# RMSNorm with swish: a ring of 100 rows instead of 96, with the last 28 rows loaded in other pieces and released by other stores

## The chip, the core and the metric

The kernel runs on one NeuronCore of one Trainium2 chip. Such a core has several engines with an instruction stream each: TensorE (not used here), VectorE (DVE in the profile), ScalarE (ACT), GpSimd (POOL) and SyncE (SP). SP does no arithmetic; here it issues the loads. ACT computes and also issues the stores. Every load and every store runs on the same 16 DMA engines, and each of the two issuing engines has a DMA queue of its own: q1 holds SP's loads, q10 holds ACT's stores. Engines wait for each other and for transfers on semaphores.

The metric is the device time in microseconds. It is given as a median over runs. A profile shows one execution.

## The reference

Each row of 512 numbers is divided by its root mean square, multiplied by `gamma`, and put through swish:

```python
batch, seq, dim = 16, 1024, 512            # x is float32
rms = np.sqrt(np.mean(x ** 2, axis=-1, keepdims=True) + eps)
x_norm = x / rms * gamma
return (x_norm * (1.0 / (1.0 + np.exp(-x_norm)))).astype(np.float32)
```

There are 16,384 rows of 2 KB. The core reads 33.56 MB and writes 33.56 MB.

## The kernel before

**Layout.** The 16,384 rows lie on 128 partitions, 128 rows to a partition. Below, "row 40" means the 41st row of every partition; one such row over all partitions is 256 KB, four of them are 1 MB, sixteen are 4 MB. The rows come in eight `groups` of 16. The buffer `xb` holds `ring` = 96 rows in each partition, that is six groups; groups 6 and 7 (rows 96 to 127) use the places of groups 0 and 1 again, which `slots` says. Everything is done in place: a row is loaded, squared, scaled, put through swish and stored from the same place.

**Loads** are twelve DMAs in SP's program order (line 119). A piece is written (group, first row in the group, number of rows). Pieces 0 to 8 fill the ring and wait for nothing: 4, 4, 8, 16, 16, 16, 16, 12 and 4 rows. The first two are issued ahead of the start barrier (`early`). Pieces 9, 10 and 11, of 16, 12 and 4 rows, go to places that were used before, so `load` makes SP wait (line 117) until the rows that stood there are stored: piece 9 waits for stores 0 and 1 (the second through `behind`), piece 10 for nothing further, piece 11 for store 2.

**Stores** are ten DMAs in ACT's program order (line 193): 16, 12, 4, then five of 16, then 8 and 8 rows. Each waits for the swish of its last rows. Two of them are also held back: `hold` makes ACT itself wait (line 191) for a landing. Store 0 stands at chunk 12 of ACT's loop and waits for load piece 7, rows 80 to 91. Store 3 stands at chunk 22 and waits for load piece 10, rows 112 to 123. Each time the four rows of one more load piece are still to come. Since the wait is an instruction of ACT's stream, everything behind it on ACT waits too.

**The computation** goes in K = 32 chunks of four rows (`cn`). For chunk k:

- ACT (`square`, lines 161 to 171) waits for the load piece that the chunk begins, squares two rows with a running sum (tile `junk`) and two rows into `sq`.
- DVE (`sums`, line 217) sums `sq`. POOL (lines 145 and 152) adds eps and takes the power of minus one half.
- DVE (`norm`, line 228) multiplies the four rows by it and by `gamma`, one row at a time.
- ACT (`swish`, line 183) applies swish to the four rows.

The order on ACT is written out by hand. In round k of its loop it issues `square(k)`, then every store that is due (two rounds after its last rows' chunk, and not before the round that `hold` names), then `swish(k - 2)`. ACT's instruction stream runs ahead of its arithmetic by a few instructions, so a store of round k can be issued while arithmetic of round k - 1 still runs.

At the end SP waits (line 250) for the stores that it has not waited for yet.

Of the kernel before, what the change touches and what calls it, by code (L numbers as in the profile page):

```python
# [9 lines left out]
def kernel(  # L10
# [8 lines left out]
    P = nc.NUM_PARTITIONS  # L19
# [6 lines left out]
    R, D = xf.shape  # L26

    groups = [16] * 8
    slots = [0, 16, 32, 48, 64, 80, 0, 16]
    loads = [(0, 0, 4), (0, 4, 4), (0, 8, 8)]  # L30
    loads += [(g, 0, 16) for g in range(1, 5)]
    loads += [(5, 0, 12), (5, 12, 4), (6, 0, 16), (7, 0, 12), (7, 12, 4)]
    stores = [(0, 0, 16), (1, 0, 12), (1, 12, 4)]
    stores += [(g, 0, 16) for g in range(2, 7)]
    stores += [(7, 0, 8), (7, 8, 8)]
    hold = {0: (loads.index((5, 0, 12)), 12), 3: (loads.index((7, 0, 12)), 22)}
    behind = {loads.index((6, 0, 16)): 1}
    ring = 96
    early = 2
    cn = 4  # L40
    n_sq = 2

    first = [sum(groups[:g]) for g in range(len(groups))]
    assert P * sum(groups) == R, R
    assert all(s + n <= ring for s, n in zip(slots, groups))

    chunks = []
    for i, (g, r, n) in enumerate(loads):
        for c in range(r, r + n, cn):
            chunks.append((slots[g] + c, i if c == r else None))  # L50
    K = len(chunks)
    assert K * cn * P == R

    ends = [-(-(first[g] + r + n) // cn) for g, r, n in stores]

    inv_d = 1.0 / float(D)
    eps_f = float(eps)
# [4 lines left out]
    def sbuf(name, shape, dt=fp32):  # L62
        return nc.alloc_sbuf_tensor(name, shape, dt).ap()

    xb = sbuf("xb", [P, ring, D])
    gamma4 = sbuf("gamma4", [P, D])
    gamma_sb = sbuf("gamma_sb", [P, D])
    neg_half = sbuf("neg_half", [P, cn])
    ms = sbuf("ms", [P, K, cn])
    aeps = sbuf("aeps", [P, K, cn])  # L70
    rstd = sbuf("rstd", [P, K, cn])
    sq = [nc.alloc_psum_tensor(f"sq{i}", [P, n_sq, D], fp32).ap() for i in range(2)]
# [20 lines left out]
    def need(ins, sem, value):  # L93
        return ins.wait_op(sem, value, "sem-ge")

    def dram(ap, piece):
        g, r, n = piece
        rows = ap[P * first[g] : P * (first[g] + groups[g])]
        return rows.rearrange("(p n) d -> p n d", n=groups[g])[:, r : r + n, :]

    def place(piece):
        g, r, n = piece
        return slots[g] + r, slots[g] + r + n

    def buf(piece):
        a, b = place(piece)
        return xb[:, a:b, :]

    stored_by_sync = set()

    def load(i):
        a, b = place(loads[i])
        for u, piece in enumerate(stores):
            c, d = place(piece)
            over = piece[0] < loads[i][0] and c < b and a < d
            if (over or behind.get(i) == u) and u not in stored_by_sync:
                nc.sync.wait_ge(st[u], 16)
                stored_by_sync.add(u)
        return nc.sync.dma_start(  # L119
            out=buf(loads[i]), in_=dram(xf, loads[i])  # L120
        ).then_inc(ld[i], 16)
# [3 lines left out]
    for t in range(early):  # L125
        ins = load(t).ins
        assert here[-1] is ins or here[-1].name == ins.name
        here.pop()
        at = next(
            i for i, other in enumerate(entry)  # L130
            if other.engine == mybir.EngineType.SP
            and isinstance(other, mybir.InstDrain)
        )
        entry.insert(at, ins)
    for t in range(early, len(loads)):
        load(t)
# [5 lines left out]
    nc.gpsimd.wait_ge(s_half, 1)  # L142
    for k in range(K):
        need(
# [11 lines left out]
        ).then_inc(s_rstd, 1)  # L156

    def square(k):
        at, landing = chunks[k]
        if landing is not None:  # L160
            nc.scalar.wait_ge(ld[landing], 16)  # L161
        for j in range(n_sq, cn):
            n = k * (cn - n_sq) + j - n_sq
            acc = nc.scalar.activation(  # L164
                out=junk[n % 2], in_=xb[:, at + j, :], func=AF.Square,
                scale=inv_d**0.5, accum_out=ms[:, k, j : j + 1],
            )
            if n >= 2:
                need(acc, s_acc, n - 1)
            acc.then_inc(s_acc, 1)  # L170
        square = nc.scalar.activation(  # L171
            out=sq[k % 2], in_=xb[:, at : at + n_sq, :],
            func=AF.Square, scale=inv_d**0.5,
        )
        if k >= 2:
            need(square, s_sum, k - 1)
        square.then_inc(s_sq, 1)

    def swish(k):
        at, _ = chunks[k]  # L180
        rows = xb[:, at : at + cn, :]
        need(
            nc.scalar.activation(out=rows, in_=rows, func=AF.Silu), s_norm, k + 1  # L183
        ).then_inc(s_swish, 1)
# [4 lines left out]
    def store(t):  # L189
        if t in hold:  # L190
            nc.scalar.wait_ge(ld[hold[t][0]], 16)  # L191
        need(
            nc.scalar.dma_start(out=dram(of, stores[t]), in_=buf(stores[t])),  # L193
            s_swish, ends[t],
        ).then_inc(st[t], 16)
# [9 lines left out]
    stored = 0  # L205
    for k in range(K + 3):
        if k < K:
            square(k)
        while stored < len(stores) and max(ends[stored] + 2, after(stored)) <= k:
            store(stored)  # L210
            stored += 1
        if 2 <= k < K + 2:
            swish(k - 2)
# [8 lines left out]
        ).then_inc(s_sum, 1)  # L222

    def norm(k):
        at, _ = chunks[k]
        for j in range(cn):
            row = xb[:, at + j, :]
            ins = nc.vector.scalar_tensor_tensor(  # L228
                out=row, in0=row, scalar=rstd[:, k, j : j + 1], in1=gamma_sb,
                op0=ALU.mult, op1=ALU.mult,  # L230
            )
            if j == 0:
                need(ins, s_rstd, k + 1)
        ins.then_inc(s_norm, 1)

    for k in range(K + 1):
        if k < K:
            sums(k)
        if k == 0:
            need(  # L240
                nc.vector.stream_shuffle(gamma_sb, gamma4, [0] * 32), s_gld, 16  # L241
            ).then_inc(s_gamma, 1)
        if k == 1:
            nc.vector.wait_ge(s_gamma, 1)
        if k >= 1:
            norm(k - 1)
# [39 lines left out]
```

## Time and profile before

| what | value |
|---|---|
| median of three runs | 160.73 us (160.39 to 161.25) |
| span of the profiled execution | 159.0 us |
| what lies around the span, median less span | 1.7 us |
| DVE busy | 124.4 us (78%) |
| ACT busy | 129.6 us (82%) |
| POOL busy | 65.4 us (41%) |
| loads, q1 | 33.56 MB, 49.8% of the 16 engines' span |
| stores, q10 | 33.57 MB, 49.2% |
| mean DMA rate over the span | 422 GB/s |

The page gives no time of the profiled execution other than its span, so the 1.7 us is the difference between the median and that span.

How to read it: a row of the page in tenths shows the busy share in 40 equal slices of 3.98 us. The chain of work is followed back from the last instruction, each step to what released it; in it, "issue" is time in which an engine waited for nothing that the profile shows, "another core or an unknown queue" is a wait whose releaser was not found, ACTq is ACT's instruction stream (here it issues DMAs), ACT its arithmetic. "DMA to landing" counts from the issue of a DMA to the moment when the last of its bytes is reported landed. In the answer on stretches of time, a DMA packet counts in the stretch in which it starts, so that short stretches can show a share over 1.

### The profile page before, as it was taken

The page shows a single profiled execution, that of the slowest core. Times are in us where ns is not written, and L with a number is a line of the kernel's source. Part 1 is how long each engine was busy: PE and PEld are TensorE (multiplying, and loading weights), DVE is VectorE, ACT ScalarE, POOL GpSimd, SP SyncE. Part 2 cuts the span into 40 slices and gives each one's busy share as a digit, 9 for nine tenths or more (in the row PEclk, how much of TensorE's full clock was granted, in tenths as well). Part 3 has the DMA queues.
Part 4 walks back from the last instruction along what each step waited for, and adds up shares of the span by engine and source line. Part 5 has one row for each costly group of instructions (what it writes and reads, how often), then busy time and mean ns, then how long its engine had stood idle before and what let it go on. Part 6 is the DMA issues. An engine that isn't in the chain of part 4 may idle for free.

```text
span 159.0 us, 507 instructions
## 1 busy us (share of the span) xinstructions
DVE 124.4 (78%) x162; ACT 129.6 (82%) x193; POOL 65.4 (41%) x71
## 2 busy tenths in 40 slices
DVE  0129999999999990299999999999999999994000
ACT  0946999999999913999999999999999999947000
POOL 2035555555555550055555555555555555550000
DMA  7999999999999999989899999999999999999997
GB/s 262 441 489 396 420 486 412 396 470 453 389 422 433 433 400 433 503 367 470 363 410 396 455 408 416 443 495 420 396 462 447 412 404 478 437 396 453 387 441 301
DMA packets 3324, 67.16 MB, mean 422 GB/s; under 512 B 500, under 2 KB 500, under 8 KB 504
## 3 DMA queue, kind: packets, MB, share of 16 engines
q1 hardware_dynamic: 1728, 33.56, 49.8%
q10 hardware_dynamic: 1592, 33.57, 49.2%
q14 instruction: 4, 0.03, 0.0%
HBM read 33.56 MB, written 33.56 MB: 422 GB/s over the span
## 4 chain that ended last, share of the span: by engine, by line
ACT 65%; DMA 12%; issue 5%; DVE 4%; ACTq 2%; another core or an unknown queue 2%; SPq 0%
ACT xb L183 27%; ACT junk L164 22%; ACT sq L171 16%; DMA xb<-in_x_dram 12%; DVE xb L228 3%; ACTq L193 2%; DVE ms L217 1%; SPq L119 0%; ACTq L191 0%; ACTq L161 0%
## 5 line engine op out<-in xcount | busy, mean ns | idle before, releaser
L228 DVE SCALAR_TENSOR_TENSOR xb<-xb,rstd,gamma_sb 128x512 f32<-128x512 f32 x128 | 87.2, 744 | 0.0
L183 ACT ACTIVATE xb<-xb 128x2048 f32<-128x2048 f32 x32 | 60.9, 1902 | 10.4 <-issue 6.3
L217 DVE TENSOR_REDUCE ms<-sq 128x2 f32<-128x1024 f32 x32 | 39.1, 1223 | 17.7 <-ACT sq L171 14.5
L145 POOL TENSOR_SCALAR aeps<-ms 128x4 f32<-128x4 f32 x32 | 20.6, 644 | 71.9 <-DVE ms L217 71.9
L152 POOL TENSOR_TENSOR rstd<-aeps,neg_half 128x4 f32<-128x4 f32 x32 | 44.0, 1376 | 2.7
L164 ACT ACTIVATE junk<-xb 128x512 f32<-128x512 f32 x64 | 37.2, 582 | 3.2 <-DMA xb<-in_x_dram 3.2
L171 ACT ACTIVATE sq<-xb 128x1024 f32<-128x1024 f32 x32 | 32.2, 1005 | 0.0
L164 ACT ACTIVATION_READ_ACCUMULATOR junk<-xb 128x1 f32 x64 | 11.9, 187 | 0.0
L204 ACT ACT_TABLE_LOAD x1 | 1.3, 1283 | 3.6 <-issue 3.6
L241 DVE LOAD_MASK_SELECT gamma_sb<-gamma x1 | 0.0, 14 | 2.8 <-DMA gamma<-in_gamma_dram 2.8
L139 POOL MEMSET blank<- 128x16 f32 x1 | 0.1, 112 | 1.5 <-POOLq L60 1.5
L241 DVE STREAM_SHUFFLE gamma_sb<-gamma 128x512 f32<-128x512 f32 x1 | 0.7, 717 | 0.0
L140 POOL MEMSET gamma<- 128x512 f32 x1 | 0.5, 524 | 0.0
L267 POOL MEMSET const-float32-0.0<- 128x1 f32 x1 | 0.1, 98 | 0.2 <-issue 0.2
L267 POOL MEMSET const-uint8-127<- 128x1 uint8 x1 | 0.1, 102 | 0.0
L267 POOL MEMSET const-bfloat16-1.0<- 128x1 bf16 x1 | 0.1, 101 | 0.0
L141 POOL MEMSET neg_half<- 128x4 f32 x1 | 0.1, 101 | 0.0
L267 POOL MEMSET const-float32-1.0<- 128x1 f32 x1 | 0.1, 98 | 0.0
## 6 DMA issues: line engine op xcount, KB each, us to landing
out_dram<-xb ACTq DMA_DIRECT2D x6, 4096.0 KB, 19.2
xb<-in_x_dram SPq DMA_DIRECT2D x5, 4096.0 KB, 28.8
xb<-in_x_dram SPq DMA_DIRECT2D x2, 3072.0 KB, 37.0
xb<-in_x_dram SPq DMA_DIRECT2D x4, 1024.0 KB, 13.3
out_dram<-xb ACTq DMA_DIRECT2D x2, 2048.0 KB, 13.0
out_dram<-xb ACTq DMA_DIRECT2D x1, 3072.0 KB, 19.0
xb<-in_x_dram SPq DMA_DIRECT2D x1, 2048.0 KB, 10.3
out_dram<-xb ACTq DMA_DIRECT2D x1, 1024.0 KB, 19.8
```

Of the source, the lines that this page charges most:

```text
L140: nc.gpsimd.memset(gamma4, 0.0).then_inc(s_zero, 1)
L145: nc.gpsimd.tensor_scalar(out=aeps[:, k, :], in0=ms[:, k, :], scalar1=eps_f, scalar2=None, op0=ALU.add,),
L152: nc.gpsimd.tensor_tensor(out=rstd[:, k, :], in0=aeps[:, k, :], in1=neg_half, op=ALU.pow),
L164: acc = nc.scalar.activation(out=junk[n % 2], in_=xb[:, at + j, :], func=AF.Square, scale=inv_d**0.5, accum_out=ms[:, k, j : j + 1],)
L171: square = nc.scalar.activation(out=sq[k % 2], in_=xb[:, at : at + n_sq, :], func=AF.Square, scale=inv_d**0.5,)
L183: nc.scalar.activation(out=rows, in_=rows, func=AF.Silu), s_norm, k + 1
L193: nc.scalar.dma_start(out=dram(of, stores[t]), in_=buf(stores[t])),
L204: nc.scalar.preload_act_table_set("silu_and_others")
L217: nc.vector.tensor_reduce(out=ms[:, k, 0:n_sq], in_=sq[k % 2], op=ALU.add, axis=mybir.AxisListType.X,),
L228: ins = nc.vector.scalar_tensor_tensor(out=row, in0=row, scalar=rstd[:, k, j : j + 1], in1=gamma_sb, op0=ALU.mult, op1=ALU.mult,)
L241: nc.vector.stream_shuffle(gamma_sb, gamma4, [0] * 32), s_gld, 16
L267: nc = _bacc.Bacc("TRN2", target_bir_lowering=False, num_devices=1)
```

## The change

The ring has 100 rows, and a row's place is its number modulo 100. Pieces of loads and stores are now written (first row, number of rows), and the code that turns a piece into places changes with that; `slots` and `chunks` are gone. What the program issues differs in this:

- Load pieces 0 to 6 are as before. Piece 7 is rows 80 to 95 (16 rows, before 12). Piece 8 is rows 96 to 99 (before 92 to 95). Both still wait for nothing. The rest is 28 rows (before 32): pieces of 12, 12 and 4 rows at 100, 112 and 124.
- Stores 0, 1 and 2 are 16, 8 and 8 rows (before 16, 12 and 4). Then come three of 16 rows as before, 16 rows (80 to 95), 4 rows (96 to 99), 12 rows (100 to 111), 8 and 8: eleven stores instead of ten.
- Load piece 9 still waits for stores 0 and 1, which are now 24 rows instead of 28; piece 11 still waits for store 2.
- Store 0 still stands at chunk 12 of ACT and waits for load piece 7, which now ends with row 95 instead of 91. Store 3 still stands at chunk 22 and waits for load piece 10, which ends with row 123 as before.

Instructions of DVE and POOL are the same. On ACT one store is added; the order of everything else stays.

```diff
-    slots = [0, 16, 32, 48, 64, 80, 0, 16]
-    loads = [(0, 0, 4), (0, 4, 4), (0, 8, 8)]
-    loads += [(g, 0, 16) for g in range(1, 5)]
-    loads += [(5, 0, 12), (5, 12, 4), (6, 0, 16), (7, 0, 12), (7, 12, 4)]
-    stores = [(0, 0, 16), (1, 0, 12), (1, 12, 4)]
-    stores += [(g, 0, 16) for g in range(2, 7)]
-    stores += [(7, 0, 8), (7, 8, 8)]
-    hold = {0: (loads.index((5, 0, 12)), 12), 3: (loads.index((7, 0, 12)), 22)}
-    behind = {loads.index((6, 0, 16)): 1}
-    ring = 96
+    ring = 100
+    loads = [(0, 4), (4, 4), (8, 8), (16, 16), (32, 16), (48, 16), (64, 16), (80, 16)]
+    loads += [(96, 4), (100, 12), (112, 12), (124, 4)]
+    stores = [(0, 16), (16, 8), (24, 8), (32, 16), (48, 16), (64, 16), (80, 16)]
+    stores += [(96, 4), (100, 12), (112, 8), (120, 8)]
+    hold = {0: ((80, 16), 12), 3: ((112, 12), 22)}
+    behind = {(100, 12): (16, 8)}
...
     def buf(piece):
-        a, b = place(piece)
-        return xb[:, a:b, :]
+        a, n = piece
+        at = a % ring
+        assert at + n <= ring, piece
+        return xb[:, at : at + n, :]
...
     def load(i):
-        a, b = place(loads[i])
-        for u, piece in enumerate(stores):
-            c, d = place(piece)
-            over = piece[0] < loads[i][0] and c < b and a < d
+        a, n = loads[i]
+        for u, (c, m) in enumerate(stores):
+            over = c + ring < a + n and a < c + m + ring
             if (over or behind.get(i) == u) and u not in stored_by_sync:
                 nc.sync.wait_ge(st[u], 16)
                 stored_by_sync.add(u)
...
     def square(k):
-        at, landing = chunks[k]
-        if landing is not None:
+        at = k * cn % ring
+        for landing in landings[k]:
             nc.scalar.wait_ge(ld[landing], 16)
```

More of the change, by code (lines that the diff above doesn't have):

```diff
@@ L43 @@
     first = [sum(groups[:g]) for g in range(len(groups))]
[L44 to L54, printed above, removed]
+    rows_each = sum(groups)
+    assert P * rows_each == R, R
+    assert ring % cn == 0
+    for pieces in (loads, stores):
+        assert [a for a, _ in pieces] == [
+            sum(n for _, n in pieces[:i]) for i in range(len(pieces))
+        ]
+        assert sum(n for _, n in pieces) == rows_each
+    K = rows_each // cn
+    hold = {t: (loads.index(piece), k) for t, (piece, k) in hold.items()}
+    behind = {loads.index(a): stores.index(b) for a, b in behind.items()}
+    landings, seen = [], 0
+    for k in range(K):
+        landings.append([])
+        while seen < len(loads) and loads[seen][0] < (k + 1) * cn:
+            landings[k].append(seen)
+            seen += 1
+    ends = [-(-(a + n) // cn) for a, n in stores]
     inv_d = 1.0 / float(D)
@@ L96, in dram @@
     def dram(ap, piece):
-        g, r, n = piece
+        a, n = piece
+        g = max(g for g in range(len(groups)) if first[g] <= a)
+        r = a - first[g]
+        assert r + n <= groups[g], piece
         rows = ap[P * first[g] : P * (first[g] + groups[g])]
         return rows.rearrange("(p n) d -> p n d", n=groups[g])[:, r : r + n, :]
-    def place(piece):
-        g, r, n = piece
-        return slots[g] + r, slots[g] + r + n
     def buf(piece):
-        a, b = place(piece)
-        return xb[:, a:b, :]
+        a, n = piece
+        at = a % ring
+        assert at + n <= ring, piece
+        return xb[:, at : at + n, :]
     stored_by_sync = set()
     def load(i):
-        a, b = place(loads[i])
-        for u, piece in enumerate(stores):
-            c, d = place(piece)
-            over = piece[0] < loads[i][0] and c < b and a < d
+        a, n = loads[i]
+        for u, (c, m) in enumerate(stores):
+            over = c + ring < a + n and a < c + m + ring
             if (over or behind.get(i) == u) and u not in stored_by_sync:
@@ L179, in swish @@
     def swish(k):
-        at, _ = chunks[k]
+        at = k * cn % ring
         rows = xb[:, at : at + cn, :]
@@ L224, in norm @@
     def norm(k):
-        at, _ = chunks[k]
+        at = k * cn % ring
         for j in range(cn):
```

## The prediction

> **What bounds the kernel now.** I read the page's slices first: which resource is busy all the time?
>
> ```profile
> span 159.0 us, 507 instructions
> DVE  0129999999999990299999999999999999994000
> ACT  0946999999999913999999999999999999947000
> DMA  7999999999999999989899999999999999999997
> ```
>
> The 16 DMA engines are busy in every slice; DVE and ACT pause near 57 to 62 us and stop near 147. So bytes set the time, as long as each next transfer is in a queue before the last one ends. The rate of a pure store stretch, from the answer on stretches (the last two numbers are DMA share and GB/s):
>
> ```profile
> 101.00:157.00 56.00, 42.63 (x56) 42.95 (x60) 21.29 (x21) 1.00 1.00 433
> 62.40:98.30 35.90, 30.96 (x40) 35.90 (x54) 16.36 (x16) 1.00 0.99 419
> ```
>
> At 433 GB/s one MB (1.049e6 bytes) takes 2.42 us and 4 MB take 9.69. The second line tells the other half: from 62.4 to 98.3 ACT is busy 35.90 of 35.90 us. In that stretch ACT has no idle time at all, so what delays its start delays its end.
>
> Next, where ACT and DMA meet. Line 191 is ACT's wait for a landing; it ended twice, at 59.0 and at 98.3. The chain of waits around both:
>
> ```profile
> L191 ACTq EVENT_SEMAPHORE  x2: 17/17/17, 59.0 to 98.3; - x2
> ...
> 55.21 0.91 ACT sq L171
> 56.12 2.88 another core or an unknown queue
> ...
> 59.08 0.34 ACTq L193
> ...
> 59.45 1.57 ACTq L193
> ...
> 61.07 1.28 ACTq L193
> ...
> 62.40 1.91 ACT xb L183
> ...
> 98.33 0.38 ACT xb L183
> ```
>
> ACT runs dry at 56.12 and waits until 59.00. That end is load 7's landing: it was issued at 4.42, and its DMA to landing is 54.6, so 59.0. Then ACT issues three stores (0.34, 1.57, 1.28 us) and computes again at 62.40. The second end of line 191, at 98.3, was not set by the DMA. The loads released near 78.5 are these two:
>
> ```profile
> L119 SPq DMA_DIRECT2D xb<-in_x_dram x2: 328/658/987, 78.5 to 78.9; - x2
> DMA to landing us min/median/max: 12.4/15.9/19.3
> ```
>
> The second, load 10, landed at 78.86 + 19.3 = 98.2. The first end shows a wait for landing ending 0.02 us after it; here it ends over 0.1 us after, together with the start of an ACT arithmetic instruction at 98.3. So ACT reached the second wait just after the landing, with nothing to spare, and store 3 went out at 98.37. Load 11 (1 MB, 2.42 us) was left in the queue; it landed at 80.90 + 19.8 = 100.7, which covered store 3's start.
>
> **The change part by part.**
>
> *ACT's first hold.* Load 7 now ends with row 95, 1 MB more ahead of the landing. Loads run at the same rate there (load 6, issued at 3.88 with 47.8 to landing, landed at 51.7 and load 7 at 59.0: 7.3 us for 3 MB), so it lands at 59.0 + 2.4 = 61.4. ACT still reaches the wait at 56.12, since everything ahead is unchanged. All of ACT behind it, and DVE and POOL which feed from ACT's squares, shift by 2.42 us: swish(10) starts at 64.8 instead of 62.40, if the three issues again take 59.08 to 62.40 = 3.3 us. Their sizes change from 12 and 4 rows to 8 and 8. The trace has no such pair there; the bounds are three quick issues (0.34 and 0.44 us as those at 98.37 and 98.75, in all about 1.2, ACT then late by only 2.42 − 2.1 = 0.3) and two at 1.57 (late by 2.7). I take 3.3 unchanged, because those are three issues in the same place in the same state of the queues.
>
> *DMA in that time.* Store 0 goes out at 61.5, with load 8 (1 MB) still in the queue as before; the DMA stays busy, cost nothing. If that cover were gone, it would cost about a start, 1 to 2 us.
>
> *Release of loads 9 to 11.* Stores 0 and 1 are 6 MB instead of 7, and start one MB later: 2.42 − 2.42 = 0, so SP is again released at about 78.4 (before, 78.49 was the first issue). But behind store 1 there is now store 2 with 2 MB (4.85 us) instead of 1 MB (2.42). Before, the stores ran out as the new loads began: store 2 landed at 61.07 + 19.8 = 80.9, and load 10, 7 MB later, at 98.2, where 7 × 2.42 = 16.96 would give 97.8. So 0.3 us or more was lost there, and I estimate at most 0.8 (the page's slices from 75.5 to 83.5 moved 363 and 410 GB/s: 93/433 × 3.98 = 0.85). The longer cover can win back between 0 and 0.8 us; I take 0.4 for load 10's landing: 97.8. SP's other waits lose nothing: load 11 needs store 2, landed near 83, while loads 9 and 10 (6 MB, 14.5 us) keep the queue full.
>
> *The second hold.* ACT's work from 62.4 to 98.3 has no idle time, and its instructions between are the same. So it comes to the wait for load 10 at 98.3 + 2.4 = 100.7; load 10 has long landed. Store 3 is issued at 98.37 + 2.42 = 100.8. Behind load 10 the DMA engines have only load 11, whose last bytes move at about 100.2 − 0.4 = 99.8 (the landing of 100.7 less about half a us for the report and the slower engines). Then the queues are empty until store 3's first bytes. This is the new stall.
>
> How long is it? The row for a DMA on idle engines is the kernel's first load, issued at 0.00:
>
> ```profile
> 0.50:1.00 0.50, 0.00 (x0) 0.00 (x0) 0.00 (x0) 1.00 0.00 0
> 1.00:1.50 0.50, 0.00 (x0) 0.00 (x0) 0.00 (x0) 1.00 1.45 246
> ```
>
> Nothing starts before 1.0 us. The load has 1 MB (2.42) and landed after 4.7 us, so 2.3 us of it are start, ramp and report. The ramp is the stretch from 1.0 to 2.0 at 246 and 197 GB/s, which loses 1 − 222/433 = 0.49 us; without it, 1.8 us.
>
> From store 3 on, 96 rows (24 MB, 58.1 us) remain to be stored in one queue. So the last landing comes at 100.8 + 1.8 + 58.1 = 160.7 without a ramp, at 161.2 with one, against 159.0: +1.7 or +2.2. The low end: if a store's start costs only its issue, 0.34 us instead of 1.0, it is +1.0. I take +1.9, between the first two, for the first load is the only row of a DMA on idle engines, but a ramp need not be the same for a store.
>
> The Trainium skill, page "DMA: Bandwidth & Descriptors", section "Specifications", puts first-byte latency on the sync and scalar path at about 0.6 us. The row above shows 1.0, and the row decides; by the page's figure the sum would be 0.4 us smaller.
>
> *After it.* No later store comes too late: the last one is issued at 146.8 + 2.4 = 149.2 and needs 2 × 2.42 + 2.3 = 7.1 us to land, 156.4, well before the end of the queue near 161; before, it took 12.2 us to land, 5 us of which were waiting. Store 6 is issued near 118.6, when the 12 MB of stores 3 to 5 last until 131. The eleventh store costs one issue of 0.34 us on ACT beside 5 us of slack: nothing. DVE and POOL ends are hidden the same way.
>
> *Sum.* +1.9 us, with nothing to add for the 0.4 us gained earlier, since store 3 waits for ACT and not for the loads. The span 159.0 becomes 160.9; with the 1.7 us around it, 162.6, or the median plus 1.9.
>
> **The rivals.**
>
> 1. *ACT is not late (not slower).* If the three issues behind the first hold are quick, 1.2 us in all instead of 3.3, ACT reaches the second wait at 98.6 and store 3 goes out at 98.7, with bytes from 99.7, when load 11 ends anyway. Then the time is 160.73 − 0.2 = 160.5, to 160.8. For it: 0.34 and 0.44 at 98.4. Against: 1.57 and 1.28 in the very place, and 0.99 for SP's second load at 78.86. It decides once the issues save over 1.5 us. Half of that saving gives 161.6.
> 2. *The mixed stretch is slow.* Store 2's 2 MB and loads 9 and 10 now run side by side for some us; the trace of before has hardly any such stretch. If load 10 landed later than 100.7, each us more would add one: at 102, 163.9. Against: it needs 3 us lost in about 10, and around 60 us, where load 8 and store 0 met, the three slices from 55.7 to 67.6 moved 400, 433 and 503 GB/s, no less than 433 in the mean. The skill's same page, section "Queues, rings and completion order", says that each DMA engine switches between queues packet by packet; that would cost order, not bytes, and no row here shows it.
> 3. *The new ring only moves bytes.* The DMA is always full and the lost 0.4 to 0.8 us comes back: 160.1. It needs ACT early as in 1, plus another us that the trace does not offer.
>
> **How the numbers follow.** About 0.5% (0.8 us) can be told from no change here. ACT late, with a hole: 80%, 161.8 to 163.2 (+1.0, and +2.2 with issues 0.3 longer), likeliest 162.6. Issues half as quick: 7%, near 161.6, on the border. Rival 1: 6%, 160.5 to 160.8. Rival 3: 3%, 160.1. Rival 2: 4%, 163.9. Slower by over 0.5% (above 161.5): 80 + 4 + half of 7, some 87; I give 0.85, since the base of 160.39 to 161.25 itself wanders. Same 0.10, faster 0.05. The range of 8 in 10 takes the ends of the unknown start and a little of the half-quick case: 161.6 to 163.4.
>
> **What would show it.** Line 191's first wait ends at 61.4, swish(10) starts near 64.8, line 191's second wait ends near 100.7, the rate falls to near zero in about 100 to 101.8, and it stays at 433 to the end. SP's first wait still ends near 78.4 and the dip at 80 is smaller. The prediction is wrong if the second hold ends near 98, or if the DMA shows no hole there.

## The result and the profile after

The changed kernel takes 162.24 us (162.15 to 162.32), the kernel before 160.56 us in the same comparison (160.18 to 161.25). The ratio is 1.0113, with a 95% interval of 1.0095 to 1.0132: slower by 1.7 us. The prediction was 162.6, range 161.6 to 163.4. The profiled execution itself took 162.3 us, with a span of 161.0.

The page of the changed kernel, its span and its slices (40 slices of 4.02 us; lines moved down by six, so line 191 is now 197, 193 is 199, 183 is 189, 119 is 125):

```profile
span 161.0 us, 509 instructions
DVE  0149979999999990099999999999999999995000
ACT  1947979999999900999999999999999999948000
DMA  7999999999999989999999997999999999999997
```

In the 15th and 16th slices (56.4 to 64.4 us) ACT has 0 and 0, where it had 1 and 3: its pause has grown. And the DMA row has a 7 in the 25th slice (96.6 to 100.6 us), where it had a 9. The account below rests on these two places. The waits at line 197 and the chain of waits around the first of them:

```profile
L197 ACTq EVENT_SEMAPHORE  x2: 17/17/17, 61.5 to 100.6; - x2
...
56.31 5.12 another core or an unknown queue
...
61.51 0.34 ACTq L199
...
61.89 1.49 ACTq L199
...
63.42 1.26 ACTq L199
...
64.72 1.91 ACT xb L189
```

The first wait ends at 61.5 instead of 59.0, since one more MB has to land; ACT's arithmetic starts again at 64.72 instead of 62.40. From there it has no gap:

```profile
64.70:100.60 35.90, 30.97 (x40) 35.88 (x54) 16.35 (x16) 1.00 0.98 409
```

It is busy for 35.88 of 35.90 us and comes to the second wait at 100.6 instead of 98.3. By then load 10 has been in place for 2 us. The same answer on stretches of 1 us shows what the DMA does meanwhile (last two numbers: DMA share and GB/s; a packet counts in the stretch in which it starts). First the kernel before, then the changed one:

```profile
98.00:99.00 1.00, 0.86 (x2) 1.00 (x2) 0.00 (x0) 1.00 1.02 434
99.00:100.00 1.00, 1.00 (x2) 1.00 (x1) 0.28 (x1) 1.00 1.69 721
100.00:101.00 1.00, 1.00 (x3) 1.00 (x4) 0.92 (x2) 1.00 0.46 197
```

```profile
99.00:100.00 1.00, 1.00 (x3) 1.00 (x5) 1.00 (x1) 1.00 0.78 328
100.00:101.00 1.00, 0.86 (x2) 1.00 (x2) 0.16 (x1) 1.00 0.06 25
101.00:102.00 1.00, 1.00 (x2) 1.00 (x1) 0.00 (x0) 1.00 1.23 524
```

Before, the big packets of the stores start from 99.6 on, on the heels of the last loads. After, the loads run out near 100, only 0.06 us of DMA work starts between 100 and 101, and the stores begin after 101. When each packet of the trace is spread evenly over its own duration, the bytes moved between 99 and 102 us are short of 433 GB/s by 1.62 us in the changed kernel and by 0.01 in the kernel before. So of the 2.0 us between the two spans this hole holds 1.6; another 0.3 is lost between 104 and 150.

### The profile page after: what moved, and what is told of

It reads as the page before. It is cut to its first block, busy times and chain, and to the rows that moved or that the text cites. A ratio compares the mean times of both kernels' runs of the same rounds, so it can differ in the third digit from the quotient of the medians.

```text
span 161.0 us, 509 instructions
## 1 busy us (share of the span) xinstructions
DVE 124.4 (77%) x162; ACT 129.6 (81%) x193; POOL 65.4 (41%) x71
## 4 chain that ended last, share of the span: by engine, by line
ACT 64%; DMA 12%; issue 5%; DVE 4%; another core or an unknown queue 3%; ACTq 2%; SPq 0%
ACT xb L189 27%; ACT junk L170 22%; ACT sq L177 16%; DMA xb<-in_x_dram 12%; DVE xb L234 3%; ACTq L199 2%; DVE ms L223 1%; SPq L125 0%; ACTq L197 0%; ACTq L167 0%
## 6 DMA issues: line engine op xcount, KB each, us to landing
xb<-in_x_dram SPq DMA_DIRECT2D x1, 2048.0 KB, 10.4
```

## The experiments

Theory A: ACT comes late to the second hold because the first hold ends 2.4 us later, and the DMA stands empty for that. Rival B: what costs the time lies in the new pieces, in the stretch where store 2 meets the loads, or in the ring.

**The first hold put back.** Ring, stores and releases stay as changed; load piece (80, 16) is cut so that the first hold can end with row 91 again.

```diff
-    loads = [..., (64, 16), (80, 16)]
-    loads += [(96, 4), (100, 12), (112, 12), (124, 4)]
+    loads = [..., (64, 16), (80, 12)]
+    loads += [(92, 4), (96, 4), (100, 12), (112, 12), (124, 4)]
-    hold = {0: ((80, 16), 12), 3: ((112, 12), 22)}
+    hold = {0: ((80, 12), 12), 3: ((112, 12), 22)}
```

> The changed kernel, with the load piece of rows 80 to 95 cut in two (80 to 91, 92 to 95) and the first hold put back on row 91; ring, stores and release of loads stay as changed. Theory A (ACT comes late to the second hold because the first hold ends 2.4 us later): the first hold ends near 59.0, the second near 98.6 on the landing of load (112, 12), no hole in the DMA, 160.4 to 160.9. Rival B (the new pieces and the stretch in which store 2 meets the loads cost the time): nothing comes back, 162.0 to 162.4.

Measured: 160.74 us against 160.46 for the kernel before in the same comparison, ratio 1.0022 (1.0008 to 1.0035). The holds end at 59.1 and 98.8. So 1.4 of the 1.7 us come back with the new ring, the new stores and the new releases all in place, and B falls, but for the remaining 0.3. The chain of waits of this run holds something that was not expected:

```profile
59.12 0.34 ACTq L199
59.50 0.44 ACTq L199
59.99 0.51 ACTq L199
60.54 1.91 ACT xb L189
```

The three issues take 1.4 us here instead of 3.2, so ACT starts again at 60.54, 1.9 us earlier than even in the kernel before. Its instruction stream then waits for load 10 at the second hold (98.7, hold over at 98.8). The run thus undoes more of ACT's lateness than the hold alone.

**The second hold one round earlier.** The first hold stays at row 95; ACT is as late as in the changed kernel, but its program comes to the second hold one chunk sooner.

```diff
-    hold = {0: ((80, 16), 12), 3: ((112, 12), 22)}
+    hold = {0: ((80, 16), 12), 3: ((112, 12), 21)}
```

> The changed kernel, with the second hold one round earlier in ACT's program (21 instead of 22); the first hold stays at row 95. Theory A: ACT's instruction stream reaches the second hold near 96.7, waits there for the landing near 98.6 while its arithmetic has work until 100.6, store 3 is issued near 98.7, the loads end near 100 and the stores follow without a hole: 160.4 to 160.9. Rival B: 162.0 to 162.4.

Measured: 160.66 against 160.46, ratio 1.0015 (1.0000 to 1.0029). The first hold ends at 61.5, ACT starts at 64.82, and the second hold ends at 98.7, with the landing. The stretches show the stores following the loads (to be read against the changed kernel's above):

```profile
99.00:100.00 1.00, 1.00 (x3) 1.00 (x5) 1.00 (x1) 1.00 0.93 393
100.00:101.00 1.00, 0.85 (x3) 1.00 (x2) 0.26 (x1) 1.00 1.29 549
```

One number in the program gives back 1.5 us. This separates the two halves of theory A: an ACT that is 2.4 us late costs no more by itself than the remaining 0.2 us (0 to 0.5 by the interval); the late store 3 costs the rest. Where the 0.2 comes from was not tested.

**A late store 3 in the kernel before.** Nothing new but the round of its second hold.

```diff
-    hold = {0: (loads.index((5, 0, 12)), 12), 3: (loads.index((7, 0, 12)), 22)}
+    hold = {0: (loads.index((5, 0, 12)), 12), 3: (loads.index((7, 0, 12)), 23)}
```

> The kernel before, with the second hold one round later (23 instead of 22), nothing else: the cost of a late store 3 by itself. Theory A: the hold ends near 102.3, the loads have ended near 100, store 3 is issued at 102.4 and the span is 102.4 + 60.24 (the distance from store 3's issue to the end in the changed kernel) = 162.6, that is 164.2 as a time. Rival B has no new pieces here: 160.6.

Measured: 164.12 (163.93 to 164.17) against 160.46, ratio 1.0229 (1.0212 to 1.0246). The old ring and the old pieces lose 3.7 us when store 3 alone is late. Its DMA stands still for the two whole microseconds after the loads:

```profile
100.00:101.00 1.00, 1.00 (x3) 1.00 (x4) 0.92 (x2) 1.00 0.06 25
101.00:102.00 1.00, 1.00 (x2) 1.00 (x3) 0.88 (x1) 1.00 0.00 0
102.00:103.00 1.00, 0.89 (x2) 1.00 (x2) 0.00 (x0) 1.00 0.00 0
```

**One issue less behind the first hold.** Store 2 goes out one round later, so that only two issues stand between the first hold and ACT's arithmetic.

```diff
-        while stored < len(stores) and max(ends[stored] + 2, after(stored)) <= k:
+        while stored < len(stores) and max(ends[stored] + 2, after(stored), {2: 13}.get(stored, 0)) <= k:
```

> The changed kernel, with store 2 issued one round later on ACT (13 instead of 12); both holds stay. Theory A: two issues instead of three stand behind the first hold, so ACT starts again near 63.4 instead of 64.7 and comes to the second hold near 99.4 instead of 100.6; the hole in the DMA shrinks from 1.7 to about 0.4 us: 160.8 to 161.2. If the lateness of ACT is not what is paid (rival B): 162.0 to 162.4. If the third issue costs ACT as much one round later: 162.0 to 162.4 too, with the second hold still at 100.6.

Measured: 161.06 against 160.30, ratio 1.0046 (1.0030 to 1.0062). ACT starts again at 63.37 and reaches the second hold at 99.3. So the time that ACT spends on issuing stores counts in the lateness like the wait itself.

Together the runs give the price of a late store 3. The first column is the end of the second hold, the last the difference of the medians of that comparison:

```
kernel                        second hold ends   against the kernel before
second hold at round 21             98.7            +0.2 us
first hold put back                 98.8            +0.3 us
store 2 one round later             99.3            +0.8 us
changed kernel                     100.6            +1.7 us
before, second hold at 23          102.6            +3.7 us
```

From 100.6 to 102.6 it is 2.0 us for 2.0 us. Between 98.8 and 100.6 it is lower (1.4 us for 1.8); that the last of the loads still covers part there is likely, but not shown. The ends of the holds come from one profiled execution each, which in the run with the first hold put back took 161.27 us against its median of 160.74. So differences of a few tenths between the upper rows mean little.

**How much store cover helps the turn to loads.** The prediction had hoped for 0.4 us from 2 MB of stores, instead of 1 MB, still queued when the loads are released (the cover, below). With the second hold at round 21 the DMA is the bound again, and a change there can show. Here load (100, 12) is released by store 0, so that 4 MB of stores are still queued; load (112, 12) is released by store 1.

```diff
-    hold = {0: ((80, 16), 12), 3: ((112, 12), 22)}
-    behind = {(100, 12): (16, 8)}
+    hold = {0: ((80, 16), 12), 3: ((112, 12), 21)}
+    behind = {}
```

> As the run with the second hold at round 21, and load (100, 12) released by store 0 alone (4 MB of stores still queued then), load (112, 12) by store 1. If the dip at the turn from stores to loads is a fixed price: as that run, 160.4 to 160.9. If it is the size of the store cover that decides it: 0.8 us less, 159.6 to 160.0. If a longer mixed stretch is slow: 161 or more.

Measured: 160.92 against 160.46, ratio 1.0033 (1.0019 to 1.0046). No gain: it is 0.3 us more than with the second hold at round 21 alone, and lies between what was expected of a fixed price and of a slow mixed stretch. The other direction, no cover at all, in the kernel before:

```diff
-    behind = {loads.index((6, 0, 16)): 1}
+    behind = {loads.index((6, 0, 16)): 2}
```

> The kernel before, with load piece 9 released by store 2 instead of store 1: no store is left in the queue when the loads are issued. Of the dip at the turn from stores to loads two readings are left. If the dip (0.9 us in the kernel before, with 1 MB of stores as a cover, and 0.9 us in the changed kernel, with 2 MB) is a price of the turn itself, it adds to the uncovered start of the loads (about 1 us from issue to first bytes, and about 0.7 for the report of store 2): 161.8 to 162.4. If the dip is only the part of the start that the cover does not hide, the whole start stands in its place, 1.7 instead of 0.9: 161.0 to 161.4.

Measured: 162.60 (162.55 to 162.72) against 160.20, ratio 1.0148 (1.0131 to 1.0165). That is 2.4 us, nearer to the additive reading and above its range. The stretch from 76 to 96 us in five kernels, in the order before (1 MB of cover), changed (2 MB), load released by store 0 (4 MB), no cover, and the first hold put back (2 MB again):

```profile
76.00:96.00 20.00, 19.41 (x26) 20.00 (x31) 10.29 (x11) 1.00 1.01 421
```

```profile
76.00:96.00 20.00, 19.38 (x26) 20.00 (x31) 10.25 (x11) 1.00 1.01 416
```

```profile
76.00:96.00 20.00, 19.38 (x26) 20.00 (x32) 10.24 (x11) 1.00 1.00 401
```

```profile
76.00:96.00 20.00, 19.42 (x26) 20.00 (x32) 10.28 (x11) 1.00 0.89 369
```

```profile
76.00:96.00 20.00, 19.42 (x26) 20.00 (x31) 10.26 (x11) 1.00 1.00 427
```

These rates have an error at their borders, since a packet counts where it starts. With each packet spread evenly over its own duration, the bytes moved between 76 and 96 us fall short of 433 GB/s by 0.87, 0.90, 1.41, 3.18 and 0.20 us. So 1 MB of cover hides most of the start of the loads, and in the changed kernel 2 MB hide no more: about 0.9 us stays. In the uncovered run the DMA stands nearly still for about 2 us, and then the loads still take some 2 us to come up to the full rate.

The last of the five does not fit a fixed price. It has the cover of the changed kernel and loses only 0.20 us here. But it loses 0.60 between 60 and 64 us, at the turn from loads to stores behind the first hold, where the kernel before loses 0.04 and the changed one 0.10. So neither turn has a price of its own in these runs, and what sets the two they do not settle.

**A more patient kernel before.** If ACT reaches the second hold with nothing to spare, the earlier round might help there too.

```diff
-    hold = {0: (loads.index((5, 0, 12)), 12), 3: (loads.index((7, 0, 12)), 22)}
+    hold = {0: (loads.index((5, 0, 12)), 12), 3: (loads.index((7, 0, 12)), 21)}
```

> The kernel before, with the second hold one round earlier (21 instead of 22). ACT was on time already, so theory A expects no change, 160.3 to 160.7; if some executions of the kernel before owe part of their time to an ACT that comes a little late, up to 0.3 us less.

Measured: 160.24 against 160.30, ratio 1.0009 (0.9983 to 1.0034): no change. None of the versions beats the kernel before.

## Why the prediction was right, and where it was not

**The first hold.** Forecast: it ends at 61.4, and swish(10) starts at 64.8. Measured 61.5 and 64.72. The three issues, taken over unchanged at 3.3 us, took 3.2. The choice was right, but the bound below it was real: with 2 MB instead of 1 MB of loads behind the hold, three issues took 1.4 us. Rival 1 had the right mechanism and a condition that the changed kernel does not meet.

**No catching up.** The step that carried the forecast, ACT busy without a gap between the holds, held: 35.88 of 35.90 us, and the second hold ended at 100.6 against a forecast of 100.7. The run with the second hold at round 21 shows that store 3's wait for this ACT is the cause and not a companion.

**The release of the loads.** Forecast: SP is released at about 78.4 as before, and load 10 lands at 97.8 instead of 98.2. SP's two loads there:

```profile
L125 SPq DMA_DIRECT2D xb<-in_x_dram x2: 328/780/1233, 78.5 to 78.9; - x2
DMA to landing us min/median/max: 12.8/16.3/19.7
```

The release is right (first issue at 78.5), the landing is not: 78.9 + 19.7 = 98.6. This is the step that failed. "The longer cover can win back between 0 and 0.8 us; I take 0.4" was worth nothing; the dip did not get smaller (0.90 us after 0.87), it moved. Store 2, 2 MB, landed at 63.42 + 20.9 = 84.3, while store 1 landed at 61.89 + 16.55 = 78.4: 5.9 us for bytes that need 4.84. The sum was not hurt, since store 3 waited for ACT anyway, as the prediction said. Rival 2's mechanism, a slow mixed stretch, did not arise: from the issue of the loads to 82.5 us only packets of the stores (q10) start. In the run with 4 MB of cover both queues ran side by side for some 11 us, at a price of 0.5 us more. The switching packet by packet that rival 2 cites does not show in the 4 us from 78.5 to 82.5, although the loads were queued already. First the changed kernel from 78.5 to 82.5, then that run from 79 to 90:

```profile
q10 hardware_dynamic: 85, 1.39, 100.3%
```

```profile
q1 hardware_dynamic: 116, 2.83, 65.1%
q10 hardware_dynamic: 112, 1.74, 36.9%
```

**The start of store 3.** Forecast: +1.7 without and +2.2 with a ramp, taken as +1.9, and 433 GB/s from there to the end. Measured: store 3 is issued at 100.70 and lands 11.1 us later. Less 9.69 us of transfer that is 1.4 us, where 1.8 was forecast without a ramp, so the term was too large by 0.4. But the rest was too small: the remaining 20 MB need 48.45 us (5 times 9.69), and end 0.7 us later than that after store 3's landing (111.83 + 48.45 = 160.28 against 160.94). In the kernel before the same difference is 0.1 (110.40 + 48.45 = 158.85 against 158.97). With the 0.2 us that the forecast had added for half a ramp, the start was too large by 0.6 and the rest too small by 0.7. That the span came out at 161.0 against a forecast of 160.9 is in this part luck. The rate shows the loss:

```profile
101.00:157.00 56.00, 44.96 (x59) 45.27 (x63) 22.49 (x22) 1.00 1.00 426
```

It is 426 instead of 433 GB/s; the hole before about 101.6 accounts for some 5 of the 7, so a little stays lost after it. It stands in one place: store 5 landed at 102.56 + 29.38 = 131.94, 10.4 us after store 4 (101.08 + 20.48 = 121.56), where 9.7 would do. The run with the first hold put back, which has no such hole, has the same 10.4 there, so the loss need not belong to store 3's lateness; its cause is open.

The start itself, in three short stretches behind the issue at 100.70:

```profile
100.70:101.20 0.50, 0.47 (x1) 0.50 (x1) 0.00 (x0) 1.00 0.00 0
101.20:101.50 0.30, 0.30 (x1) 0.30 (x1) 0.00 (x0) 1.00 0.00 0
101.50:101.80 0.30, 0.30 (x1) 0.30 (x1) 0.00 (x0) 1.00 4.12 1748
```

No packet starts before 101.5, and then all 16 engines start within 0.3 us. The first packet starts at 101.54, 0.84 us after the issue: nearer to the 1.0 us of the kernel's first load than to the 0.6 us that the Trainium skill, page "DMA: Bandwidth & Descriptors", section "Specifications", gives. What the store does not have is the load's ramp.

**The time as a whole.** The medians differ by 1.7 us, the spans by 2.0; around the span of the profiled execution lie 1.3 us (162.3 − 161.0), where 1.7 were carried over from the kernel before. That is the 0.4 us between the forecast of 162.6 and 162.24. The term of 1.7 was mis-sized: it took a median of three executions less the span of one. In all executions on record with both numbers, of every kernel here, the time is 1.26 to 1.36 us above the span, so the profiled execution of the kernel before must have taken about 160.3, less than the 160.73.

**After it.** The last store was issued at 149.14 and landed 11.8 us later: the 5 us of slack at the end were there, and the eleventh store cost nothing visible.

## What to carry to other kernels

A wait that is written into the instruction stream of a computing engine is paid twice: once where it stands, and again at every later place where that engine must come in time, until some stretch has idle time to give back. Look for the next meeting of the two resources and ask how much the engine has to spare there; here it was nothing, and 2.4 us of delay became 1.7 us of time, most of it an empty queue. The cure was not to remove the wait but to place the next issue one round earlier in the program, which brought back 1.5 us.

## What the runs showed that was not expected

- The issue of a store on ACT has no fixed price. The second and third of a burst took 1.49 and 1.26 us in the changed kernel, but 0.44 and 0.51 us where 2 MB of loads were still queued behind the hold. With store 2 a round later, the first two issues at the second hold took 0.34 and 1.66 us. The long ones stand where the stores have just begun to flow; what makes them long was not tested.
- The turn of the DMA engines from stores to loads lost about 0.9 us in the kernel before (1 MB of stores queued behind the release) and in the changed one (2 MB), 1.4 with 4 MB, and 3.2 with none, in which the empty time is included. With the first hold put back it lost 0.2 with 2 MB, while the earlier turn from loads to stores lost 0.6 instead of 0.1.
- A store on idle DMA engines needed 1.4 us beyond its bytes (11.1 less 9.69, for 4 MB; 11.1 again in the kernel before with its second hold at round 23), the kernel's first load 2.3 (4.7 less 2.42, for 1 MB).
